# Seven block products in place of eight in the first SwiGLU product, its input normalized beforehand and its result sent through DRAM

## The chip, the cores and the metric

One core of one Trainium2 chip. TensorE (PE) multiplies 128x128 tiles, VectorE (DVE), ScalarE (ACT) and GpSimd (POOL) do the elementwise work, SyncE (SP) issues the DMAs. The metric is the device time of one execution in microseconds (us); lower is better. One median is given for several runs, and one more execution was profiled.

## What is computed

One step of a decoder layer for 1024 prompt positions and 8 sample positions, 1032 columns in all (T). The part that matters is its second half, the feed-forward network behind the mixer, all in float32:

```python
# Layer: x -> x + RMSNorm_post(Mixer(RMSNorm_pre(x))) -> h + RMSNorm_post(SwiGLU(RMSNorm_pre(h)))
def swiglu(x, w_ffn_in, w_ffn_out):
    hcat = x @ w_ffn_in                                  # 1024 -> 2 * 2816
    gate, up = hcat[..., :FFN_HIDDEN], hcat[..., FFN_HIDDEN:]
    return (jax.nn.silu(gate) * up) @ w_ffn_out          # 2816 -> 1024

yp = yp + rmsnorm(mix, norm_mix_post[l])
yp = yp + rmsnorm(swiglu(rmsnorm(yp, norm_ffn_pre[l]), w_ffn_in[l], w_ffn_out[l]), norm_ffn_post[l])
```

## The kernel before

Everything lies transposed: the 1024 model features are 8 tiles of 128 partitions (`KT`), the 1032 positions are columns. To keep float32 accuracy every operand is split into a high part and a low part (`hi`, and `lo = x - hi`, both in the type fp32r), and each product is three matmuls: high by high, weight low by input high, weight high by input low. The splits are done by ACT (the cast, line 156) and DVE (the subtraction, line 157).

The 2816 hidden features are 22 tiles (`HT`). For hidden tile t, `ffn_in` computes a gate product `pg` and an up product `pu`, each a sum over 8 feature tiles times 3 matmuls, for three column chunks `CH` of 344. That is 2 x 8 x 3 x 3 = 144 matmuls of 344 columns for a tile. The evacuation scales both by the column's norm factor `rf` (the input `fh`, `fl` is not divided by the norm; the factor is applied behind the product), takes silu, multiplies, and splits the result into `hh` and `hl` in on-chip memory. After each group of six tiles (the last has four) `ffn_out` multiplies them by the output weights and adds to `fac`; so first and second product alternate.

Ahead of this stands the stage of the norms: for each column chunk, the attention part of the mixer's output projection is added to `mix`; a sum of squares over partitions (the `nps` matmul with `ones`, followed by a square root on ACT and a reciprocal on DVE, line 191) gives the norm; `mix` becomes h, goes to `h_d`, and a second sum of squares gives `rf`. For chunk 2 the state-space part of the projection (eight `gemm` calls with `cc=(2,)`) comes first. POOL does part of the multiplications, of the sums and of the weight splits here.

The order of instructions on each engine is fixed when the program is built: by the priorities `prio(...)` and a scheduler; each engine then runs its own queue strictly in that order and waits at semaphores. SP issues all DMAs in one queue, among them 91 copies of about 1 MB from the key/value caches to the outputs, handed out by `next_copy` at the pace `RATE`.

## Time and profile before

| | |
|---|---|
| runs: median (lowest to highest of 3) | 1928.76 us (1927.81 to 1932.84) |
| the profiled execution's own time | 1929.59 us |
| its span in the trace | 1927.8 us |
| lying around the span | 1.8 us |
| granted clock of TensorE, mean | 0.979 |
| busy TensorE, VectorE, ScalarE, GpSimd | 95%, 53%, 38%, 20% of the span |

The span runs from the first to the last instruction of the trace. Matmuls are pipelined, so a matmul's own duration is longer than the distance from its start to the next one's start; it is this distance that adds up, and the text calls it the step of a matmul. A granted clock of 1.00 is 2.4 GHz, 0.50 is 1.2 GHz.

### The profile page before, as it was taken

How to read it: one execution, taken by the hardware profiler on the slowest of the kernel's cores; microseconds unless marked ns; L12 is line 12 of the kernel's file. 1: busy time of each engine (PE TensorE's matmuls, PEld its weight loads, DVE VectorE, ACT ScalarE, POOL GpSimd, SP SyncE). 2: the span in 40 equal slices, each digit the busy share in tenths (PEclk: the TensorE clock that was granted, in tenths of full speed). 3: DMA queues.
4: the chain of work that ended last, by engine and by line, in shares of the span. 5: the costliest groups of instructions: out<-in, count | busy, mean ns of one | idle time of the engine just before them, and what ended most of it. 6: DMA issues, size and time to landing. Idle time of an engine off the chain costs nothing. (4 is left out here: it accounts for less than half of the span.)

```text
span 1927.8 us, 29260 instructions
## 1 busy us (share of the span) xinstructions
PE 1825.0 (95%) x11727; PEld 1709.3 (89%) x11727; DVE 1014.0 (53%) x1896; ACT 739.2 (38%) x1388; POOL 394.5 (20%) x277
## 2 busy tenths in 40 slices
PE   8999989999999899998879989999999999999994
PEld 6999878888888798887679989999999999999993
DVE  6544676757764544455774896331333333333348
ACT  5543554545554455665242353222221112211242
POOL 0000244543232311133533342000000000000025
PEclk9999999999999999999889999999999999999997
DMA  4322333443334433464754454347433643366362
GB/s 162 122 95 86 119 108 112 137 128 107 104 115 136 156 100 110 142 237 137 178 154 133 147 168 132 109 150 249 133 115 130 240 164 131 105 202 207 115 247 88
DMA packets 125544, 275.26 MB, mean 143 GB/s; under 512 B 17616, under 2 KB 83632, under 8 KB 124000
## 3 DMA queue, kind: packets, MB, share of 16 engines
q1 hardware_dynamic: 125408, 273.39, 43.4%
q8 instruction: 92, 1.51, 0.3%
q14 instruction: 44, 0.36, 0.1%
HBM read 235.86 MB, written 125.47 MB: 187 GB/s over the span
## 5 line engine op out<-in xcount | busy, mean ns | idle before, releaser
L168 PE MATMUL g<-xh,wh 128*128 128x344 f32 x1344 | 443.7, 330 | 9.7 <-ACT zt L893 5.5
L168 PE MATMUL g<-xl,wh 128*128 128x344 f32 x1344 | 440.4, 328 | 1.5 <-DVE xl L222 1.5
L168 PE MATMUL g<-xh,wl 128*128 128x344 f32 x1344 | 439.0, 327 | 0.5 <-DVE wl L157 0.5
L168 PEld LDWEIGHTS g<-xh,wh 128*128 128x128 f32 x1344 | 255.8, 190 | 19.3 <-ACT zt L893 6.1
L168 PEld LDWEIGHTS g<-xh,wl 128*128 128x128 f32 x1344 | 256.2, 191 | 11.3 <-issue 9.9
L168 PEld LDWEIGHTS g<-xl,wh 128*128 128x128 f32 x1344 | 256.3, 191 | 10.4 <-issue 7.4
L157 DVE TENSOR_TENSOR wl<-wr,wh 128x1024 fp32r<-128x1024 f32 (+1 forms) x133 | 163.0, 1226 | 124.9 <-ACT wh L156 124.7
L156 ACT CAST wh<-wr 128x1024 fp32r<-128x1024 f32 (+1 forms) x133 | 134.4, 1011 | 214.5 <-PE g L168 128.8
L168 PE MATMUL pg<-fh,wl 128*128 128x344 f32 x504 | 161.8, 321 | 0.2 <-DVE wl L157 0.2
L168 PE MATMUL pg<-fl,wh 128*128 128x344 f32 x504 | 161.8, 321 | 0.0
L168 PE MATMUL pu<-fl,wh 128*128 128x344 f32 x504 | 161.6, 321 | 0.0
L168 PE MATMUL pu<-fh,wh 128*128 128x344 f32 x504 | 161.2, 320 | 0.0
L168 PE MATMUL pu<-fh,wl 128*128 128x344 f32 x504 | 160.8, 319 | 0.0
L168 PE MATMUL pg<-fh,wh 128*128 128x344 f32 x504 | 158.5, 322 | 0.0
L1110 POOL TENSOR_TENSOR ow<-wr,ow 128x512 fp32r<-128x512 f32 x8 | 11.1, 1407 | 674.9 <-ACT ow L1109 674.9
L168 PE MATMUL g<-hl,wh 128*128 128x344 f32 x432 | 138.0, 319 | 0.0
L168 PE MATMUL g<-hh,wl 128*128 128x344 f32 x432 | 137.6, 319 | 0.0
L168 PE MATMUL g<-hh,wh 128*128 128x344 f32 x432 | 137.3, 320 | 0.0
L230 DVE TENSOR_TENSOR u<-pu,rf 128x344 f32<-128x344 f32 x66 | 34.1, 516 | 195.5 <-PE pu L168 195.5
L650 ACT ACTIVATE sm<-sm,ngm 128x128 f32<-128x128 f32 (+1 forms) x192 | 84.9, 443 | 108.3 <-DVE ngm L646 106.2
L606 POOL TENSOR_TENSOR sw<-sw,sin 128x1032 f32<-128x1032 f32 x24 | 74.9, 3122 | 247.6 <-ACT sw L605 184.1
L1079 ACT CAST hh<-s 128x344 fp32r<-128x344 f32 x66 | 31.7, 480 | 199.4 <-DVE s L1078 197.3
(323 smaller groups left out, 3710.7 us busy)
## 6 DMA issues: line engine op xcount, KB each, us to landing
out_skv<-in_cache SPq DMA_DIRECT2D x64, 1023.5 KB, 5.3
wr<-in_w_in SPq DMA_DIRECT2D x56, 512.0 KB, 3.8
wr<-in_w_fin SPq DMA_DIRECT2D x44, 512.0 KB, 3.8
out_skv<-in_cache SPq DMA_DIRECT2D x16, 1022.0 KB, 5.5
wr<-in_w_out SPq DMA_DIRECT2D x24, 512.0 KB, 4.1
wr<-in_w_fout SPq DMA_DIRECT2D x24, 384.0 KB, 4.2
e<-cs_d SPq DMA_DIRECT2D x16, 512.0 KB, 3.9
n_d<-nh SPq DMA_DIRECT2D x12, 512.0 KB, 4.2
```

Source lines behind the costliest of these rows:

```text
L156: nc.scalar.copy(wh[:, :cols], wr[:, :cols])
L157: nc.vector.tensor_tensor(out=wl[:, :cols], in0=wr[:, :cols], in1=wh[:, :cols], op=ALU.subtract)
L168: nc.tensor.matmul(ps, x[:, ws], y[:, c0:c1], start=(k == 0 and j == 0), stop=(k == n - 1 and j == 2))
L230: return nc.vector.tensor_tensor(out=dst, in0=ps, in1=r[:dst.shape[0], c0:c1], op=ALU.mult)
L606: nc.gpsimd.tensor_tensor(out=sw[:, 0:T], in0=sw[:, 0:T], in1=sin, op=ALU.mult)
L650: nc.scalar.activation(out=sm[:, h, :nk], in_=sm[:, h, :nk], func=AF.Exp, scale=SCALE, bias=ngm[:, g, j, i:i + 1], accum_out=den[:, g, j, ...
L1079: nc.scalar.copy(hh[:, c0:c1], s)
L1110: nc.gpsimd.tensor_tensor(out=wl, in0=src, in1=wh, op=ALU.subtract)
```

## The change

Tiles 0 and 1 keep the plain products (`plain`). For tiles 2 to 21 the 2 x 2 block product (gate and up rows, lower and upper half of the features, two neighbouring column blocks A and B of `HB` = 258) is done by a scheme with seven block products instead of eight: b11, b21, t2, b22, t3, t4, t1. Each is 4 feature tiles x 3 matmuls of 258 columns, and it is done for two column halves s, so a tile is 7 x 12 x 2 = 168 matmuls of 258 columns. The scheme needs sums of input blocks and of weight blocks. The input's sums are made once, in place in `mix` (`x_sums`, `x_last`). The weights' sums are made for each tile (`w_blocks`): four sums of 512 columns, and three and a half splits instead of two. The seven results are combined by adds while they leave PSUM (`blocks`), over eight banks in turn.

For that the input has to be normalized before the product, so `Norms` divides by the second norm first, and `fh`, `fl` are made after it; `GAP` says behind how many units of TensorE's work the two norm matmuls of a chunk stand. POOL has no part in the norms any more. The result of a tile goes to DRAM (`hid_d`); `hid_load` fetches and splits it for the second product, whose four groups now stand together at the end. `RATE` for the cache copies goes from 0.52 to 0.43; 76 of them are handed out in the feed-forward part, as before.

```diff
 NEG = -1e30
 SCALE = 0.125
 
@@ -112,6 +114,12 @@
...
-    h_d = [dtile(f"h_d{k}", [P, T]) for k in range(KT)]
+    h_d = dtile("h_d", [KT, P, T])
+    hid_d = [dtile(f"hid_d{t}", [P, T]) for t in range(HT)]
...
-    for c, (c0, c1) in enumerate(CH):
-        if c == 2:
...
+    class Norms:
+
+
+        def __init__(self, c):
+            self.c0, self.c1 = CH[c]
+            self.acc = np_.tile([P, CW], F32, tag="nacc", name="nacc")
+
+        def part(self, m, ps):
+            mv = mix[m][:, self.c0:self.c1]
+            r = nc.vector.tensor_tensor(out=mv, in0=mv, in1=ps, op=ALU.add)
+            stat(mv, m == 0, self.acc)
+            return r
...
+        def first(self, prev):
+            c0, c1 = self.c0, self.c1
+            with prio("evac"):
+                r = np_.tile([P, CW], F32, tag="nr", name="nr", bufs=1)
+                finish(self.acc, r, prev=prev)
...
+                    self.h += [x[:, j] for j in range(n)]
+                    for m in range(3 * i, 3 * i + n):
+                        mv, h = mix[m][:, c0:c1], self.h[m]
+                        nc.vector.tensor_tensor(out=mv, in0=mv, in1=r, op=ALU.mult)
+                        nc.vector.scalar_tensor_tensor(out=h, in0=mv, scalar=nw(MIX_POST, m), in1=h, op0=ALU.mult,
+                                                       op1=ALU.add)
+                        stat(h, m == 0, self.acc)
+                    nc.sync.dma_start(out=h_d[3 * i:3 * i + n, :, c0:c1].rearrange("k p t -> p k t"), in_=x[:, :n])
...
+        def second(self, prev):
+            c0, c1 = self.c0, self.c1
+            with prio("evac"):
+                r = np_.tile([P, CW], F32, tag="nr", name="nr2", bufs=1)
+                finish(self.acc, r, prev=prev)
+                for m in range(KT):
+                    mv = mix[m][:, c0:c1]
+                    nc.vector.scalar_tensor_tensor(out=mv, in0=self.h[m], scalar=nw(FFN_PRE, m), in1=r, op0=ALU.mult,
+                                                   op1=ALU.mult)
+                    nc.scalar.copy(fh[m][:, c0:c1], mv)
+                    nc.vector.tensor_tensor(out=fl[m][:, c0:c1], in0=mv, in1=fh[m][:, c0:c1], op=ALU.subtract)
+
...
+    def att_part(c):
+        nm = Norms(c)
         for m in range(KT):
...
             ps = gps()
-            unit(ps, [x[:, (m % 2) * 512:(m % 2 + 1) * 512] for x in pair], ahs, als, c)
+            last = unit(ps, [x[:, (m % 2) * 512:(m % 2 + 1) * 512] for x in pair], ahs, als, c)
             with prio("evac"):
-                ev(c, ps)
+                nm.part(m, ps)
+            step(last, .5)
+        ahead.extend([(GAP[c][0], nm.first), (GAP[c][1], nm.second)])
+
+    att_part(0)
+    att_part(1)
+    for m in range(KT):
+        step(gemm(a["w_out"][m][:, 512:1536], 1024, sh, sl, ssm_ev(m), cc=(2,), share=True))
+    att_part(2)
+    right.close()
...
+    def plain(t, c, w):
+        c0, c1 = CH[c]
...
-    fst = ExitStack()
-    hhp = pool(fst, "hhp", 6, side="right")
-    hlp = pool(fst, "hlp", 6, side="right")
-    tmp = pool(fst, "tmp", 2, side="right")
+            s = np_.tile([P, T], F32, tag="fs", name="fs", bufs=2)[:, :CW]
+            nc.scalar.activation(out=s, in_=pg, func=AF.Silu)
+            next_copy(nc.vector.tensor_tensor(out=s, in0=s, in1=pu, op=ALU.mult))
+            nc.sync.dma_start(out=hid_d[t][:, c0:c1], in_=s)
+        step(last, 2)
...
+    def x_raw(s):
+        a0 = 2 * s * HB
+        A, B = slice(a0, a0 + HB), slice(a0 + HB, a0 + 2 * HB)
+        half[s, "b11"] = [(fh[k][:, A], fl[k][:, A]) for k in range(4)]
+        half[s, "b21"] = [(fh[4 + k][:, A], fl[4 + k][:, A]) for k in range(4)]
+        half[s, "b22"] = [(fh[4 + k][:, B], fl[4 + k][:, B]) for k in range(4)]
+
...
+        with prio("evac"):
+            for k in range(4):
+                x, y = mix[k], mix[4 + k]
+                nc.vector.tensor_tensor(out=x[:, A], in0=x[:, B], in1=x[:, A], op=ALU.subtract)
+                nc.vector.tensor_tensor(out=x[:, B], in0=y[:, B], in1=x[:, B], op=ALU.subtract)
+                nc.vector.tensor_tensor(out=y[:, B], in0=y[:, B], in1=x[:, A], op=ALU.subtract)
+                nc.vector.tensor_tensor(out=y[:, A], in0=y[:, A], in1=y[:, B], op=ALU.subtract)
+            split("t2", 4, B)
+            split("t3", 0, B)
+            split("t4", 4, A)
+
+    def x_last(s):
+
+        a0 = 2 * s * HB
+        A, B = slice(a0, a0 + HB), slice(a0 + HB, a0 + 2 * HB)
+        with prio("evac"):
+            for k in range(4):
+                nc.scalar.copy(fh[k][:, B], mix[k][:, A])
+                nc.vector.tensor_tensor(out=fl[k][:, B], in0=mix[k][:, A], in1=fh[k][:, B], op=ALU.subtract)
+        half[s, "t1"] = [(fh[k][:, B], fl[k][:, B]) for k in range(4)]
...
+    wslots = [(mixp, "mix")] * 8 + [(whp, "wh"), (wlp, "wl"), (whp, "wh"), (wlp, "wl")]
...
+    banks = [(psg, "g"), (psa, "ap"), (pss, "sp"), (pst, "ap"), (psg, "g"), (psa, "ap"), (pss, "sp"), (psn, "ap")]
...
+            def slot():
+                p, tag = wslots[nws[0] % len(wslots)]
+                nws[0] += 1
+                return p.tile([P, 1024 if p in (whp, wlp) else T], F32R, tag=tag, name="wsl")
+
+            def split(n0, n1, x):
+                wh, wl = slot(), slot()
+                nc.scalar.copy(wh[:, :1024], x)
+                nc.vector.tensor_tensor(out=wl[:, :1024], in0=x, in1=wh[:, :1024], op=ALU.subtract)
+                res[n0] = (wh[:, :512], wl[:, :512])
+                res[n1] = (wh[:, 512:1024], wl[:, 512:1024])
...
+            split("b11", "b21", g)
+            nc.vector.tensor_tensor(out=s1, in0=a21, in1=a22, op=ALU.add)
+            sub(s2, s1, a11)
+            split("t1", "t2", sa[:, :1024])
+            sub(s3, a11, a21)
+            sub(s4, a12, s2)
+            split("t3", "b22", sb[:, :1024])
+            w = slot()
+            nc.scalar.copy(w[:, :512], a22)
+            nc.vector.tensor_tensor(out=w[:, 512:1024], in0=a22, in1=w[:, :512], op=ALU.subtract)
+            res["t4"] = (w[:, :512], w[:, 512:1024])
+        return res
...
+    def blocks(t, s, w):
+        def prod(name):
...
+            with prio("main"):
+                for k, (hi, lo) in enumerate(half[s, name]):
+                    ks = slice(k * P, (k + 1) * P)
+                    for j, (x, y) in enumerate(((wh, hi), (wl, hi), (wh, lo))):
+                        nc.tensor.matmul(ps, x[:, ks], y, start=(k == 0 and j == 0), stop=(k == 3 and j == 2))
+            return ps
...
+        p = np_.tile([P, 4, HB], F32, tag="xr", name="fp", bufs=3)
+        o_ = np_.tile([P, 4, HB], F32, tag="fs", name="fo", bufs=2)
+        p1, u2, v, u3 = (p[:, i] for i in range(4))
+        gate, up = o_[:, 0:2], o_[:, 2:4]
+        b = prod("b11")
+        with prio("evac"):
+            nc.scalar.copy(p1, b)
+        b = prod("b21")
+        with prio("evac"):
...
+        b = prod("t1")
+        with prio("evac"):
+            add(gate[:, 1], v, b)
+            add(up[:, 1], u3, b)
+            nc.scalar.activation(out=gate, in_=gate, func=AF.Silu)
+            nc.vector.tensor_tensor(out=up, in0=up, in1=gate, op=ALU.mult)
+            nc.sync.dma_start(out=hid_d[t][:, 2 * s * HB:(2 * s + 2) * HB], in_=up.rearrange("p i t -> p (i t)"))
...
-    def ffn_weights(t, far):
-        if not far:
...
-    def ffn_in(ts, order):
...
-            with prio("evac"):
-                s = tmp.tile([P, LW], F32, tag="s", name="s")[:, :CW]
-                u = tmp.tile([P, LW], F32, tag="u", name="u")[:, :CW]
-                scaled(s, pg, c, rf)
-                last = nc.scalar.activation(out=s, in_=s, func=AF.Silu)
-                scaled(u, pu, c, rf)
-                nc.vector.tensor_tensor(out=s, in0=s, in1=u, op=ALU.mult)
-                nc.scalar.copy(hh[:, c0:c1], s)
-                nc.vector.tensor_tensor(out=hl[:, c0:c1], in0=s, in1=hh[:, c0:c1], op=ALU.subtract)
-                next_copy(last)
...
+    hslots = [(tx, "tx")] * 12 + [(actp, "act")] * 16
...
+    def hid_load(t):
+        with prio("w"):
+            hr = np_.tile([P, T], F32, tag="xr", name="hr", bufs=3)
+            nc.sync.dma_start(out=hr, in_=hid_d[t])
...
+                res.append(p.tile([P, T], F32R, tag=tag, name=f"h{'hl'[i]}{t}"))
+            nc.scalar.copy(res[0], hr)
+            nc.vector.tensor_tensor(out=res[1], in0=hr, in1=res[0], op=ALU.subtract)
+        hid[t] = res
...
+    pw = [(load_w(a["w_fin"][0], 1024), load_w(a["w_fin"][HT], 1024)), (far_weights(1), far_weights(HT + 1))]
+    for t, c in ((0, 0), (0, 1), (1, 0), (1, 1)):
+        plain(t, c, pw[t])
+    assert not ahead
+    for s in range(2):
+        x_raw(s)
+        x_sums(s)
+    for t in range(2):
+        plain(t, 2, pw[t])
+    for s in range(2):
+        x_last(s)
+    for t in range(2, HT):
+        w = w_blocks(t)
+        for s in range(2):
+            blocks(t, s, w)
+    fac = [mixp.tile([P, T], F32, tag="mix", name=f"fac{m}") for m in range(KT)]
     for gi, (t0, t1) in enumerate(groups):
-        if gi == 0:
-
-            ffn_in((0, 1), [(0, 0), (0, 1), (1, 0), (1, 1), (0, 2), (1, 2)])
-        for t in range(2 if gi == 0 else t0, t1):
-            ffn_in((t,), [(t, c) for c in range(3)])
+        for t in range(t0, t1):
+            hid_load(t)
         ffn_out(gi)```

What the build makes of it on the engines, at three places.

The first is VectorE's queue within one hidden tile, well inside the first product. Before, `s` and `u` are the scaled gate and up products, `wl` a weight split, `hl` the split of the result; these rows are one column chunk with the weights of the next tile:

```order
L230 TENSOR_TENSOR s<-pg,rf 128x344
L157 TENSOR_TENSOR wl<-wr,wh 128x1024
L230 TENSOR_TENSOR u<-pu,rf 128x344
L1078 TENSOR_TENSOR s<-s,u 128x344
L157 TENSOR_TENSOR wl<-wr,wh 128x1024
L1080 TENSOR_TENSOR hl_13421<-s,hh_13420 128x344
```

Now, about half a tile of the same queue: `fb` is a block product in PSUM, `fp` and `fo` the partial results, `sa` and `sb` the weight sums, `wsl` a weight split:

```order
L1211 TENSOR_TENSOR fp<-fp,fb 128x258 x3
L1185 TENSOR_TENSOR sa<-wu 128x512
L1182 TENSOR_TENSOR sb<-wg,wu 128x512
L1177 TENSOR_TENSOR wsl<-wg,wsl 128x1024
L1211 TENSOR_TENSOR fo<-fp,fb 128x258
L1182 TENSOR_TENSOR sa<-sa,wg 128x512
L1211 TENSOR_TENSOR fo<-fp,fb 128x258 x2
L1182 TENSOR_TENSOR sb<-wg,sa 128x512
L1211 TENSOR_TENSOR fo<-fp,fb 128x258
L1177 TENSOR_TENSOR wsl<-sa,wsl 128x1024
L1240 TENSOR_TENSOR fo<-fo 128x516
```

The work on a tile's weights stands between the adds of another tile's products, one to two tiles ahead of its use.

The second is TensorE's queue at the last norm matmul, the second one of chunk 2 (`nps`). Before, it stands in an up product of tile 1 (`wxh`, `wxl` are that tile's weights), and nothing but the scaling of results needs it:

```order
L168 MATMUL pu<-fh_10005,wxh_10991 128x344
L168 MATMUL pu<-fh_10005,wxl_10992 128x344
L990 MATMUL nps<-nacc_10878,ones 128x344
L168 MATMUL pu<-fl_10013,wxh_10991 128x344
L168 MATMUL pu<-fh_10006,wxh_10991 128x344
```

Now it stands inside the gate product of tile 1 for chunk 1, after 18 of its 24 matmuls:

```order
L176 MATMUL pg<-fl_10027,wxh 128x344
L1001 MATMUL nps<-nacc_10980,ones 128x344
L176 MATMUL pg<-fh_10020,wxh 128x344
L176 MATMUL pg<-fh_10020,wxl 128x344
L176 MATMUL pg<-fl_10028,wxh 128x344
```

Behind it in the queue are the rest of that unit, its up product, and the four units of chunk 2, whose input needs this norm.

The third is VectorE's queue ahead of that matmul, whose operand `nacc_10980` is the sum of squares of h. In the kernel before the same stretch holds splits and products, and no sums of input blocks:

```order
L1024 SCALAR_TENSOR_TENSOR fl_10013<-mix_9518,par,fh_10005 128x344
L1078 TENSOR_TENSOR s<-s,u 128x344
L1024 SCALAR_TENSOR_TENSOR fl_10014<-mix_9519,par,fh_10006 128x344
L230 TENSOR_TENSOR s<-pg,rf 128x344
L1080 TENSOR_TENSOR hl_10999<-s,hh_10998 128x344
L230 TENSOR_TENSOR u<-pu,rf 128x344
L191 RECIPROCAL rf<-rf 128x344
```

Now the splits of the first half's sums (`xt2`, `xt3`, `xt4`) stand between its first and its last six adds:

```order
L1127 TENSOR_TENSOR xt3l<-mix_9528,xt3h 128x258
L997 TENSOR_TENSOR nacc_10980<-nacc_10980,sq 128x344
L1127 TENSOR_TENSOR xt3l<-mix_9529,xt3h 128x258
L1127 TENSOR_TENSOR xt3l<-mix_9530,xt3h 128x258
L1127 TENSOR_TENSOR xt4l<-mix_9531,xt4h 128x258
L1127 TENSOR_TENSOR xt4l<-mix_9532,xt4h 128x258
L1127 TENSOR_TENSOR xt4l<-mix_9533,xt4h 128x258
L1127 TENSOR_TENSOR xt4l<-mix_9534,xt4h 128x258
L997 TENSOR_TENSOR nacc_10980<-nacc_10980,sq 128x344 x6
L1103 TENSOR_TENSOR fs<-fs,pu 128x344 x2
L201 RECIPROCAL nr_11136<-nr_11136 128x344
```

So the norm of chunk 2 stands behind the block sums of the first half in VectorE's queue.

## Rows read from the trace of the kernel before

**Rows 1.** the page: span, and TensorE's busy time with its share and instructions
```profile
span 1927.8 us, 29260 instructions
...
PE 1825.0 (95%) x11727; PEld 1709.3 (89%) x11727; DVE 1014.0 (53%) x1896; ACT 739.2 (38%) x1388; POOL 394.5 (20%) x277
```

**Rows 2.** the chain of waits: start us, length us, engine, tile, line, instructions
```profile
1193.35 3.78 PE pg L168 x24
...
1283.92 67.74 PE g L168 x432
...
1849.43 23.36 PE g L168 x132
```

**Rows 3.** busy time by stretch (the first line names the columns)
```profile
core 0: us, PE busy (x) PEld busy (x) DVE busy (x) ACT busy (x) POOL busy (x), PEclk, DMA share, GB/s
1048.00:1194.00 146.00, 133.61 (x800) 130.13 (x799) 120.91 (x154) 66.28 (x113) 57.44 (x41) 0.96 0.47 151
1194.00:1284.00 90.00, 90.00 (x574) 90.00 (x574) 32.03 (x55) 18.43 (x32) 0.00 (x0) 1.00 0.31 105
...
1849.00:1928.00 79.00, 51.09 (x297) 49.24 (x295) 56.60 (x75) 30.12 (x57) 36.38 (x31) 0.82 0.48 181
```

**Rows 4.** timeline of TensorE at the end: start us, us, instruction
```profile
1879.98 0.34 PE L168 MATMUL g<-hl,ow 128*128 128x388 f32 x1
...
1883.68 0.34 PE L168 MATMUL g<-hl,ow 128*128 128x388 f32 x1
...
1891.00 0.80 PE L168 MATMUL g<-hh,ow 128*128 128x256 f32 x2 [4.15 <-DVE fac L1123]
...
1897.46 0.28 PE L168 MATMUL g<-hl,ow 128*128 128x256 f32 x1
...
1902.74 0.28 PE L168 MATMUL g<-hl,ow 128*128 128x256 f32 x1
1913.14 1.22 PE L990 MATMUL nps<-facc,ones 128*128 128x256 f32 x2 [10.12 <-DVE facc L1129]
```

**Rows 5.** busy time of TensorE in two stretches (x: matmuls), granted clock last but two
```profile
1897.46:1902.74 5.28, 5.28 (x47) 1.00 0.00 0
1891.60:1895.44 3.84, 3.84 (x19) 0.50 0.45 155
```

**Rows 6.** groups by line and shape: us busy, ns of one, idle before
```profile
L157 DVE TENSOR_TENSOR wl<-wr,wh 128x1024 fp32r<-128x1024 f32 x109 | 140.0, 1284 | 74.7 <-ACT wh L156 74.5
...
L156 ACT CAST wh<-wr 128x1024 fp32r<-128x1024 f32 x109 | 114.4, 1049 | 110.6 <-PE g L168 38.9 <-PE pu L168 37.8 <-PE pg L168 33.1
...
L1080 DVE TENSOR_TENSOR hl<-s,hh 128x344 fp32r<-128x344 f32 x66 | 34.4, 521 | 22.9 <-ACT hh L1079 22.9
...
L458 DVE TENSOR_TENSOR hs<-hs,tm 128x512 f32<-128x512 f32 x16 | 11.0, 690 | 13.2 <-POOL tm L454 13.2
...
L190 ACT ACT_TABLE_LOAD x4 | 5.1, 1283 | 0.1
```

**Rows 7.** timeline of VectorE in the stage of the norms
```profile
1070.06 0.92 DVE L1001 TENSOR_TENSOR mix<-mix,g 128x344 f32<-128x344 f32 x2
...
1071.88 2.29 DVE L191 RECIPROCAL nr<-nr 128x344 f32<-128x344 f32 x1
...
1157.70 4.58 DVE L1020 TENSOR_TENSOR mix<-mix,nr 128x344 f32<-128x344 f32 x4
1162.20 1.54 DVE L1021 SCALAR_TENSOR_TENSOR mix<-mix,par,xr 128x344 f32<-128x344 f32 x3
```

**Rows 8.** timeline of VectorE at the end
```profile
1900.70 0.74 DVE L1123 TENSOR_TENSOR fac<-fac,g 128x256 f32<-128x256 f32 x2
```

**Rows 9.** what TensorE waited for from 1050 to 1195: us, times, longest
```profile
PE nps L990 <- POOL nacc L986: 3.2, 1, 3.2
```

**Rows 10.** DMA issues from 1194 on: count, KB, median us to landing
```profile
wr<-in_w_fin SPq DMA_DIRECT2D x36, 512.0 KB, 3.6
...
hres<-h_d SPq DMA_DIRECT2D x8, 516.0 KB, 9.7
```

More of the change, by code (lines that the diff above doesn't have):

```diff
@@ L977, in trunk, with stat @@
     fl = [actp.tile([P, T], F32R, tag="act", name=f"fl{k}") for k in range(KT)]
-    rf = rowp.tile([P, T], F32, tag="row", name="rf")
-    def stat(x, first, acc, eng):
+    def stat(x, first, acc):
         if first:
@@ L983, in stat, with finish @@
         else:
-            sq = np_.tile([P, CW], F32, tag="sq", name="sq")
+            sq = np_.tile([P, T], F32, tag="fs", name="sq", bufs=2)[:, :CW]
             nc.scalar.activation(out=sq, in_=x, func=AF.Square)
-            eng.tensor_tensor(out=acc, in0=acc, in1=sq, op=ALU.add)
-    def finish(acc, dst, cw=CW):
+            nc.vector.tensor_tensor(out=acc, in0=acc, in1=sq, op=ALU.add)
+    def finish(acc, dst, cw=CW, prev=None):
         sp_ = side_ps("nps")
-        nc.tensor.matmul(sp_[:, :cw], ones, acc, start=True, stop=True)
+        ins = nc.tensor.matmul(sp_[:, :cw], ones, acc, start=True, stop=True)
+        if prev is not None:
+            behind(ins, prev)
@@ L998, in trunk, with step @@
+    ahead = []
+    def step(last, n=1):
+        ahead[:] = [(k - n, f) for k, f in ahead]
+        while ahead and ahead[0][0] <= 0:
+            ahead.pop(0)[1](last)
+    def att_part(c):
+        nm = Norms(c)
         for m in range(KT):
-            def ev(c, ps, m=m, acc=acc):
-                r = nc.vector.tensor_tensor(out=mix[m][:, c0:c1], in0=mix[m][:, c0:c1], in1=ps, op=ALU.add)
-                stat(mix[m][:, c0:c1], m == 0, acc, nc.vector)
-                return r
             if m % 2 == 0:
```

147 lines of the change are left out of this document (90 added, 57 removed).

## The prediction, made blind

> **What bounds the kernel now.** I read the page first: TensorE is busy for 95% of a span of 1927.8 us [rows 1]. A high busy share alone proves little, because matmul durations overlap; so next comes the chain of waits. From 1193.35 to 1849.43, where the first and second products alternate, it consists of TensorE alone: two units of 24 matmuls after each other without a gap, then 432 matmuls in 67.74 us, and so on [rows 2]. The busy time by stretch says the same: from 1194 to 1284 TensorE is busy 90.00 of 90 us at clock 1.00, VectorE only 32 of 90 [rows 3]. So each matmul taken out of the first product is worth its step, as long as nothing else becomes late. The two stages around it are different. From 1048 to 1194, the stage of the norms, TensorE has holes and VectorE is busy for 121 of 146 us. The end, from 1849 on, hangs on VectorE and GpSimd [rows 3, 4].
>
> **What the product costs, before and after.** Four tiles took from 1193.35 to 1283.92 us [rows 2]: 90.57 us, 22.64 us a tile, which is 0.157 us for each of 144 matmuls of 344 columns. The change runs 168 matmuls of 258 columns. There is no row with 258, but there are neighbours at full clock. With 388 columns, 21 steps lie between 1879.98 and 1883.68: 0.176 us each. With 256, 45 steps lie between 1897.46 and 1902.74: 0.1173 us each [rows 4]; the clock there is 1.00 [rows 5]. The slope between them is 0.446 ns a column, and it gives 0.1566 for 344, which fits. So 258 columns cost 0.1182 us and a tile 19.86 us. Twenty tiles: 397.2 instead of 452.9 us, a **gain of 55.7 us**. That is nearly the full eighth, because almost the whole step goes with the columns.
>
> A fixed cost for each matmul would speak against more and shorter matmuls. The rows leave about 3 ns of it. The Trainium skill (TensorE: Matmul & The Clock Gate, Part 3, The mechanism) says that a weight load runs beside a matmul only when the two use different row groups, which full 128-row loads never do. By that rule every step would carry its load and the seven products would win far less or lose; the trace does not agree, since a step of 0.1173 us with a load each shows the load covered.
>
> **Does VectorE keep up in a tile?** Its queue for one tile holds 14 adds from PSUM of 258 columns (0.37 us each back to back [rows 8], for 256), two multiplications of 516 and four weight sums of 512 (0.69 [rows 6]), three splits of 1024 (1.28 [rows 6]) and one of 512 (0.69): 5.2 + 1.4 + 2.8 + 3.8 + 0.7 = 13.9 us of 19.9. ScalarE has 3.5 casts (1.05 each [rows 6]), two copies and two silus, under 7 us. The weight work stands one to two tiles ahead in the queue, and eight banks hold 8 x 1.43 us of results, so I put the edit's sums, splits and adds at nothing: TensorE covers them. Without that cover each microsecond over 19.9 costs 20 us. The two loads of a tile land in 3.6 us [rows 10], once in 20 us.
>
> **The stage of the norms.** Here the change adds to the engine that is already short. Up to the first norm of chunk 0 the queues are the same; its reciprocal starts at 1071.88 [rows 7], and one add more stands ahead of it: 1072.4. From it to the first weight split of tile 2 (`wsl<-wg`) I count VectorE's queue: 109 two-operand instructions of 344 columns (0.46 us back to back [rows 7]) 50.1 us; 48 with a scalar (0.51 [rows 7]) 24.5; 60 of 258 columns, nearly all block sums and their splits (0.37 [rows 8]) 22.2; 13 weight splits of 1024 (1.28 [rows 6]) 16.6; 6 reciprocals (2.29 [rows 7]) 13.7; 4 weight sums (0.69) 2.8. Sum 129.9 us, so 1202.3 without any wait. The mean step matters: before, multiplications cost 4.58 us for four while GpSimd ran [rows 7]; now GpSimd is out of the norms, and I take the undisturbed step.
>
> The waits: VectorE's second reciprocal of chunk 1 waits for its `nps`, which stands behind the first units of tile 0, about 2.7 us. The last `nps` waits for the six adds behind the block sums; 101 of the 129.9 us lie up to them, so they are done near 1176. TensorE arrives near 1159: the weights of tile 0 are split near 1129, three pairs of units of 7.5 us and 18 matmuls follow, and the input of chunk 1 holds it for some 4 us. So TensorE stands for some 17 us, where before its wait at such a matmul was 3.2 us [rows 9]. It loses its clock for the next few us (at clock 0.50 a step of 256 columns was 3.84/18 = 0.213 [rows 5]), and behind the `nps` ScalarE needs two table loads (1.28 each [rows 6]) and a square root before the reciprocal: 3 us more. Then chunk 2 is normalized (12 us), TensorE follows with its four units, and the second half's sums run beside them. First block product at about 1202.3 + 2.7 + 3 = **1208** instead of 1193.4: **14.6 us lost**. The bounds: 1201, if the waits lie beside each other, and 1220, if the waits cost as much again as TensorE lacked in this stage before (133.6 of 146 us busy [rows 3], 12.4).
>
> **The way through DRAM.** Stores go out beside the products. When the last tile ends, hidden tiles 0 and 1 are already split; the load of tile 5 waits for a buffer, lands some 4 us later (a load of this size took 3.6 to 9.7 [rows 10]), and its split (1.05 + 1.28) is done 9 us after the end. TensorE has 5.5 us of work with tiles 0 and 1 in five open units, and 2.4 us with each further one. I take **3 us** of holes, between 0 and 9. Later groups load ahead. Before, the two products alternated and this seam did not exist.
>
> **The end.** The second product's last group is the same (78.4 us from 1849.43 to the span's end). The residual's tiles 4 to 7 can only be loaded when `ow` buffers come free, so some adds of chunk 0 move behind those of chunk 2. The hole of 4.15 us that they made [rows 4] shrinks, and they come back between 1902.74 and the last `nps` at 1913.14. I take 0, between -4 and +5.
>
> **Sum** against the profiled execution's own 1929.6 us: -55.7 + 14.6 + 3 + 0 = -38.1, so **1891 us**, 2.0% below; the median of the runs, 1928.8, is 0.8 lower than that execution.
>
> **The rivals.** *A lighter transition* (15%): the norms stage ends by 1201 or sooner, because GpSimd no longer slows VectorE, and the end gains its 4 us. Time 1929.6 - 55.7 + 8 + 3 - 4, about 1881. For it: GpSimd was busy for 57 of the 146 us of that stage [rows 3]. *A heavier transition or small holes in every tile* (20%): the stage ends at 1220 and 0.3 us a tile is lost at banks or casts: 1929.6 - 55.7 + 27 + 6 + 3, about 1910. For it: the weight splits already waited 74.7 us for ScalarE's casts [rows 6], and four stand in each tile's queue now. *VectorE becomes the bound of the first product* (5%), slower than before: every split at the head of VectorE's queue waits for a cast, and that for a slot that a later product frees, so the adds behind it hold the banks. It decides from 19.86 + 38/20 = 21.8 us a tile; at 22.5 the time is 1891 + 53 = 1944. Against it: 13.9 us of work. *The step does not shrink with the columns* (2%): 168 x 0.157 = 26.4 us a tile, 1891 + 20 x 6.5 = 2021. The 256-column steps speak against it; the skill's rule on loads named above would push this way. *Nothing visible* (3%): gain and seams cancel, 1929.
>
> **From these to the numbers.** The main case has 55% and its own range 1883 to 1900. The range 1872 to 1912 takes in the lighter case and the heavier one up to a little beyond its time; it leaves out the far side of the heavier case, the three last rivals and a little below, some 2 in 10. Within 0.3% means within 5.8 us of the median, about what a measurement of this kernel can tell. Faster: main, lighter and heavier cases, 0.90; same 0.03; slower 0.07.
>
> **What would show it.** In the changed profile: `fb` matmuls of 258 columns, 3360 of them in 397 us without gaps (a tile 19.9 us); VectorE busy about 70% there; a hole of TensorE at an `nps` of more than 10 us, released by VectorE's `nacc`; the first `fb` at about 1208; and from the last `fb` to the end some 285 us (3 + 3 x 67.7 + 78.4). I am wrong if the `fb` stretch is much longer than 400 us with TensorE waiting for `wsl` or for banks, or if the stage of the norms ends beyond 1220.

## The result, and the profile after the change

The changed kernel takes **1903.3 us** (median of 4 runs, 1900.4 to 1907.3) against 1928.3 for the kernel before in the same session: ratio 0.987, 95% interval 0.984 to 0.989. It is 25.0 us faster, 1.3%; 38 were forecast. The profiled execution is the slowest of the four, 1907.3 us with a span of 1905.4. Its page, whose lines answer to [rows 1]:

```profile
span 1905.4 us, 30773 instructions
...
PE 1781.1 (93%) x12207; PEld 1662.1 (87%) x12207; DVE 1148.8 (60%) x2223; ACT 783.9 (41%) x1436; POOL 350.0 (18%) x242
```

480 matmuls more than before, 44 us less of busy TensorE. The chain of waits of the changed kernel (start, length, engine, tile or table load, line, instructions), from the end of the norms on, answers to [rows 2]:

```profile
1184.52 1.28 ACT L1102
1185.82 0.47 ACT fs L1102
1186.33 4.66 PE pg L176 x18
1190.99 0.58 PE nps L1001 x2
...
1217.82 403.18 PE fb L1207 x3357
...
1639.70 208.00 PE g L176 x1305
...
1866.68 0.58 PE g L176 x3
1867.26 9.36 DMA hres<-h_d
...
1890.64 1.23 PE nps L1001 x2
```

The twenty tiles are one piece of 403.18 us on TensorE alone. Ahead of it and at the end the chain changes engines every few microseconds, through ScalarE, VectorE and a load. Busy time by stretch (columns as in [rows 3]), the stage of the norms, the block products and the seam:

```profile
1150.00:1218.00 68.00, 43.22 (x233) 40.74 (x232) 58.76 (x132) 33.23 (x71) 0.00 (x0) 0.82 0.28 95
1218.00:1621.00 403.00, 403.00 (x3359) 403.00 (x3359) 263.13 (x480) 113.78 (x162) 0.00 (x0) 1.00 0.51 175
1621.00:1640.00 19.00, 18.03 (x113) 17.46 (x113) 11.06 (x12) 11.04 (x15) 0.00 (x0) 1.00 0.93 291
```

What TensorE waited for in the changed kernel (us in total, times, longest), two rows of the norms and one of the end:

```profile
PE pg L176 <- ACT fs L1102: 18.4, 1, 18.4
PE nps L1001 <- DVE nacc L997: 1.5, 1, 1.5
...
PE nps L1001 <- DVE facc L1309: 15.7, 2, 15.4
```

The long wait of the norms is not at the last `nps`. It stands at a plain unit (`pg`) that waits for a silu on ScalarE.

From these rows the difference of the two profiled executions adds up (spans, 1905.4 - 1927.8 = -22.4):

| part | before | after | forecast | measured |
|---|---|---|---|---|
| to the first norm's reciprocal | 1071.9 | 1076.5 | +0.5 | +4.6 |
| from it to the steady block products | 121.5 | 141.3 | +14.1 | +19.8 |
| twenty tiles | 452.9 | 403.2 | -55.7 | -49.7 |
| seam through DRAM | none | 1.0 | +3 | +1.0 |
| the end (the rest) | | | 0 | +1.9 |

The reciprocals of VectorE in the changed kernel from which the first rows come, the first one of the stage and the second one of chunk 1:

```profile
1076.48 2.30 DVE L201 RECIPROCAL nr<-nr 128x344 f32<-128x344 f32 x1
...
1148.94 2.30 DVE L201 RECIPROCAL nr<-nr 128x344 f32<-128x344 f32 x1
```

The first row of the table is scatter of the program ahead of the change. In the traces of the experiments whose code up to there does the same, that reciprocal starts between 1067.0 and 1076.3; the profiled execution is late in it. That may be most of its 4 us over its own median; the other executions have no trace that would show it.

### The profile page after: what moved, and what is told of

Its sections match the earlier page's. It is cut to its first block, busy times and chain, and to the rows that moved or that the text cites. A ratio compares the mean times of both kernels' runs of the same rounds, so it can differ in the third digit from the quotient of the medians.

```text
span 1905.4 us, 30773 instructions
## 1 busy us (share of the span) xinstructions
PE 1781.1 (93%) x12207; PEld 1662.1 (87%) x12207; DVE 1148.8 (60%) x2223; ACT 783.9 (41%) x1436; POOL 350.0 (18%) x242
## 4 chain that ended last, share of the span: by engine, by line
PE 36%; DVE 8%; DMA 4%; issue 1%; ACT 1%; POOL 1%; SPq 0%; DVEq 0%; POOLq 0%; ACTq 0%
PE fb L1207 21%; PE g L176 14%; DMA nt<-n_d 2%; PE pg L176 1%; POOL nt L856 1%; DVE xr L1034 1%; DVE nacc L997 1%; DVE wl L165 1%; DMA hres<-h_d 0%; DMA hr<-hid_d 0%; PE pu L176 0%; DVE fac L1330 0%; DMA cvt<-in_cache 0%; DVE mix L1046 0%; DVE nt L858 0%
## 5 line engine op out<-in xcount | busy, mean ns | idle before, releaser
L176 PE MATMUL g<-xh,wh 128*128 128x344 f32 x1344 | 443.7, 330 | 4.7 <-ACT rw L587 3.4
L176 PE MATMUL g<-xl,wh 128*128 128x344 f32 x1344 | 441.1, 328 | 1.5 <-DVE xl L232 1.5
L176 PE MATMUL g<-xh,wl 128*128 128x344 f32 x1344 | 439.7, 327 | 0.5 <-DVE wl L165 0.5
L176 PEld LDWEIGHTS g<-xh,wh 128*128 128x128 f32 x1344 | 256.2, 191 | 14.1 <-ACT rw L587 5.7
L176 PEld LDWEIGHTS g<-xh,wl 128*128 128x128 f32 x1344 | 256.5, 191 | 13.2 <-issue 11.8
L176 PEld LDWEIGHTS g<-xl,wh 128*128 128x128 f32 x1344 | 256.8, 191 | 9.7 <-issue 6.8
L1207 PE MATMUL fb<-fh,wsl 128*128 128x258 f32 x1280 | 234.6, 283 | 0.9 <-DVE wsl L1177 0.7
L1207 PEld LDWEIGHTS fb<-fh,wsl 128*128 128x128 f32 x1280 | 198.0, 189 | 1.5 <-DVE wsl L1177 0.9
L1207 PE MATMUL fb<-fl,wsl 128*128 128x258 f32 x640 | 180.8, 283 | 0.0
L165 DVE TENSOR_TENSOR wl<-wr,wh 128x1024 fp32r<-128x1024 f32 (+1 forms) x93 | 111.7, 1201 | 83.8 <-ACT wh L164 83.5
L176 PE MATMUL g<-hh,wh 128*128 128x344 f32 x432 | 137.4, 320 | 0.7 <-ACT wh L164 0.7
L176 PE MATMUL g<-hh,wl 128*128 128x344 f32 x432 | 137.7, 319 | 0.2 <-DVE wl L165 0.2
L176 PE MATMUL g<-hl,wh 128*128 128x344 f32 x432 | 137.3, 320 | 0.0
L1289 POOL TENSOR_TENSOR ow<-wr,ow 128x512 fp32r<-128x512 f32 x8 | 10.1, 1296 | 684.8 <-ACT ow L1288 684.8
L164 ACT CAST wh<-wr 128x1024 fp32r<-128x1024 f32 (+1 forms) x93 | 92.6, 996 | 102.0 <-PE g L176 94.9
L1207 PEld LDWEIGHTS fb<-fl,wsl 128*128 128x128 f32 x640 | 120.9, 189 | 0.0
L616 ACT COPY sw<-rw 32x1032 f32<-32x1032 f32 x96 | 101.1, 1053 | 1.4
L1211 DVE TENSOR_TENSOR fo<-fp,fb 128x258 f32<-128x258 f32 x160 | 63.9, 421 | 58.0 <-PE fb L1207 55.6
L587 ACT COPY rw<-g 128x344 f32<-128x344 f32 x108 | 47.3, 444 | 112.2 <-PE g L176 72.0
L176 PEld LDWEIGHTS g<-hh,wh 128*128 128x128 f32 x432 | 80.9, 188 | 1.1 <-ACT wh L164 1.0
## 6 DMA issues: line engine op xcount, KB each, us to landing
out_skv<-in_cache SPq DMA_DIRECT2D x64, 1023.5 KB, 5.6
wr<-in_w_in SPq DMA_DIRECT2D x56, 512.0 KB, 3.7
wr<-in_w_out SPq DMA_DIRECT2D x24, 512.0 KB, 3.7
hr<-hid_d SPq DMA_DIRECT2D x22, 516.0 KB, 4.8
wg<-in_w_fin SPq DMA_DIRECT2D x20, 512.0 KB, 5.4
wu<-in_w_fin SPq DMA_DIRECT2D x20, 512.0 KB, 3.5
```

The source lines that it names most:

```text
L164: nc.scalar.copy(wh[:, :cols], wr[:, :cols])
L165: nc.vector.tensor_tensor(out=wl[:, :cols], in0=wr[:, :cols], in1=wh[:, :cols], op=ALU.subtract)
L176: last = nc.tensor.matmul(ps, x[:, ws], y[:, c0:c1], start=(k == 0 and j == 0), stop=(k == n - 1 and j == 2))
L587: return nc.scalar.copy(rw[:, c0:c1], ps)
L616: nc.scalar.copy(sw[q * 32:(q + 1) * 32, 0:T], rw[s * 32:(s + 1) * 32, :])
L1207: nc.tensor.matmul(ps, x[:, ks], y, start=(k == 0 and j == 0), stop=(k == 3 and j == 2))
```

## The experiments

The scatter is as large as some effects. So the experiments are read in two intervals of their traces, measured from inside: from the second reciprocal of chunk 1 to the start of the last block product (471.8 us in the changed kernel: 1148.94 to 1620.70), and from there to the end of the span (284.7). These intervals scatter too: the changed kernel and e1, whose code is the same up to the last block product, differ by 0.9 us in the first; the changed kernel, e2, e3, e6 and e9, whose code is the same in the end, lie between 282.3 and 284.7 in the second (e7, at 289.1, is told below). All are edits of the changed kernel.

| run | to the last block product | from it to the end | median us | ratio to before (95%) |
|---|---|---|---|---|
| changed kernel | 471.8 | 284.7 | 1903.3 | 0.987 (0.984 to 0.989) |
| e1, residual's buffers | 472.7 | 281.0 | 1897.8 | 0.985 (0.983 to 0.988) |
| e2, sums behind the norm | 472.2 | 283.5 | 1902.2 | 0.987 (0.985 to 0.988) |
| e3, sums on GpSimd | 468.3 | 284.0 | 1900.2 | 0.986 (0.984 to 0.987) |
| e8, four mends | 467.0 | 273.7 | 1889.3 | 0.980 (0.978 to 0.982) |
| e9, squares apart | 468.2 | 282.3 | 1897.7 | 0.984 (0.982 to 0.985) |
| e11, mends with GpSimd | 462.4 | 275.8 | 1885.8 | 0.976 (0.974 to 0.979) |
| e12, mends without | 460.7 | 273.8 | 1881.1 | 0.975 (0.972 to 0.978) |

**Order of the sums (e2).** All of them stay on VectorE; those of the first half move behind the norm of chunk 2 (`behind` sets the order on one engine).

```diff
-                nc.vector.tensor_tensor(out=x[:, A], in0=x[:, B], in1=x[:, A], op=ALU.subtract)
+                behind(nc.vector.tensor_tensor(out=x[:, A], in0=x[:, B], in1=x[:, A], op=ALU.subtract), order[0])
...
```

> Only the order on VectorE changes: the input sums of the first half stand behind the second norm of chunk 2 instead of ahead of its last adds. Theory A (VectorE's whole work up to the first block product decides, wherever the sums stand): the last nps comes some 10 us earlier, near 1181, but the 10.1 us of sums then stand between it and the first weight split; first block product again at 1213 to 1219, time within 5 us of 1905. Theory B (the sums hurt only because they stand ahead of those adds; behind them TensorE's four units of chunk 2 cover them): first block product near 1207, time about 1895.

Measured: 0.4 us longer to the last block product. The last `nps` in the chain of this run, and TensorE's wait at the first weight splits:

```profile
1178.85 0.59 PE nps L1001 x2
```
```profile
PE fb L1207 <- ACT wsl L1176: 8.1, 2, 7.6
```

The last `nps` stands 33.0 us behind the second reciprocal of chunk 1 (1145.89 here) instead of 42.0, so it came 9 us sooner; and TensorE lost 8.1 of them again at the first weight split, whose buffers (`mix`, the first eight of `wslots`) are free only when all sums are done. The forecast's way of counting, the whole queue of VectorE up to that split, holds; its place in the queue only moves the hole.

**The sums on GpSimd (e3).** `eng` is GpSimd for the first half, VectorE for the second.

```diff
-        a0 = 2 * s * HB
+        eng, a0 = (nc.vector if s else nc.gpsimd), 2 * s * HB
...
-                nc.vector.tensor_tensor(out=x[:, A], in0=x[:, B], in1=x[:, A], op=ALU.subtract)
+                eng.tensor_tensor(out=x[:, A], in0=x[:, B], in1=x[:, A], op=ALU.subtract)
...
```

> The input sums of the first half and their low parts move from VectorE to GpSimd, which does nothing from 1150 to 1218; the casts of these sums stand behind the squares of chunk 2 on ScalarE. Theory A (VectorE's work up to the first block product decides): 10.1 us leave VectorE, the last nps comes near 1181, the first block product near 1208, time about 1897. Theory B (GpSimd beside VectorE slows it down as much as it takes off, as with the four multiplications that took 4.58 us): first block product at 1215 or later, time 1903 to 1908.

Measured: 3.5 us shorter, a third of the 10.1 us taken off. The same eight multiplications on VectorE, in the changed kernel with GpSimd idle:

```profile
1166.94 3.51 DVE L1033 TENSOR_TENSOR mix<-mix,nr 128x344 f32<-128x344 f32 x8
```

and in this run with GpSimd's adds beside them:

```profile
1160.44 6.97 DVE L1033 TENSOR_TENSOR mix<-mix,nr 128x344 f32<-128x344 f32 x8
```

They took twice the time. And a part was lost on ScalarE: the last `nps` came 32.5 us behind the second reciprocal of chunk 1 (1175.91), 9.4 sooner than in the changed kernel, but behind it ScalarE had casts of the sums, silus and two table loads to do before the square root:

```profile
1176.37 1.28 ACT L1102
...
1180.93 1.28 ACT L200
1182.23 0.56 ACT nr L200
```

So the reciprocal started 6.9 us behind that `nps`, in the changed kernel 1.4. Both theories are part of it: VectorE's work decides, and GpSimd takes back much of what it takes off; ScalarE's order, which neither names, takes its share.

**Squares in places of their own (e9).** The code has two buffers (`fs`) in turn for the squares of the norms and for the silus of the plain tiles. Here the squares of chunk 2's second norm go elsewhere.

```diff
-                        stat(h, m == 0, self.acc)
+                        stat(h, m == 0, self.acc, fl[m][:, c0:c1] if c1 == T else None)
...
```

> The squares of chunk 2's second norm are written into the part of the low input tiles that is still unused, one place each (rounded to the format of those tiles), instead of into the two buffers that they share with the silus of the plain tiles. Theory A (sharing these two buffers puts the silus behind all squares on ScalarE, and so holds the banks of TensorE's next units): the wait of 18.4 us for a silu goes, TensorE does its 7.5 us of units ahead of the last nps, which follows the last add; the first block product comes 62 to 65 us after the second reciprocal of chunk 1 instead of 68.9; time about 1898. Theory B (VectorE's adds end last anyway, and the units only change places with the wait): 67 us or more, time 1902 to 1905.

Measured: 3.6 us shorter. The 68.9 us run from 1148.94 to 1217.82 in the changed kernel, from where its last block product starts 402.9 us later; the first interval less 402.9 us is the count for the other runs, and it gives 65.3 here, at the far end of theory A's 62 to 65; time 1897.7. On ScalarE the two silus now start at 1164.95, ahead of the squares (in the changed kernel at 1185.82):

```profile
1164.95 0.81 ACT L1102 ACTIVATE fs<-pg 128x344 f32<-128x344 f32 x2 [6.29 <-PE pg L176]
```

TensorE's timeline has the hole where I had forecast it:

```profile
1185.66 1.51 PE L1001 MATMUL nps<-nacc,ones 128*128 128x344 f32 x2 [10.16 <-DVE nacc L997]
```

So in the changed kernel the banks were held by silus that stood behind squares for a buffer, and 5 us of plain units (4.66 us in the chain above) came behind the hole instead of into it.

**The residual's buffers (e1).** In the forecast I had the late loads wait for `ow` buffers. The chain says otherwise: the load of 9.36 us starts behind the group's last matmul (`PE g`, 1866.68), since `hres` 4 to 7 reuse the buffers of hidden tiles 20 and 21.

```diff
-                h = actp.tile([P, T], F32, tag="act", name=f"hres{m}")
+                h = (actp.tile([P, T], F32, tag="act", name=f"hres{m}") if m < 4 else tx.tile([P, T], F32, tag="tx", name=f"hres{m}"))
```

> Only the buffers of the residual's tiles 4 to 7 change: they no longer reuse those of hidden tiles 20 and 21, which the very last matmul still reads, but those of tiles 14 and 15, free one group earlier. Theory A (the late loads make the end longer): the wait of 9.36 us for a residual tile leaves the chain, the hole ahead of the last nps shrinks from 15.4 us to 6 to 9, and the execution gets 6 to 9 us shorter, about 1896 to 1898. Theory B (VectorE's own work bounds the end, busy 43.7 of the last 58 us, and the wait only fills a pause): less than 3 us. The stage of the norms and the block products stay as they are, first block product near 1218.

Measured: 3.7 us less in the end (1.3 less than the shortest end without the edit), between the two theories; the hole ahead of the last `nps` went from 15.4 to 10.5. The rest has another cause, and two timelines of this run show it, VectorE and GpSimd with four multiplications each:

```profile
1845.58 4.64 DVE L1330 TENSOR_TENSOR fac<-fac,fr 128x388 f32<-128x388 f32 x4
```
```profile
1844.87 4.93 POOL L1330 TENSOR_TENSOR fac<-fac,fr 128x388 f32<-128x388 f32 x4 [28.63 <-DVE fr L201]
```

**256 columns (e4).** This run, a single execution, is for the step alone.

```diff
-                        nc.tensor.matmul(ps, x[:, ks], y, start=(k == 0 and j == 0), stop=(k == 3 and j == 2))
+                        nc.tensor.matmul(ps, x[:, ks], y[:, :256], start=(k == 0 and j == 0), stop=(k == 3 and j == 2))
...
```

> Every block product is computed for 256 of its 258 columns; the last two columns of each block are left out (and set to zero), so that matmuls have the width of the row from which I took the step. Theory A (the step goes with the columns at 0.45 ns each, and the row of 45 steps was a quicker place): step 0.119 us, the 3360 matmuls take 400 us instead of 403.2. Theory B (258 columns cost something that 256 do not): step 0.1173 as in that row, 394 us.

Its chain:

```profile
1217.63 400.21 PE fb L1207 x3357
```

0.1192 us a step: theory A. A matmul of 256 columns costs 1.6% more in this stretch than the 0.1173 of [rows 4]; the two columns more cost 0.0009. Why the two places differ I didn't find out; both have the granted clock 1.00.

**More work for VectorE in the product (e6, e7).** The three large weight splits of a tile are made two or three times; each run is a single execution.

```diff
-                nc.vector.tensor_tensor(out=wl[:, :1024], in0=x, in1=wh[:, :1024], op=ALU.subtract)
+                for _ in range(2):
+                    nc.vector.tensor_tensor(out=wl[:, :1024], in0=x, in1=wh[:, :1024], op=ALU.subtract)
```

> In every tile of the block products VectorE makes each of the three large weight splits twice, with the same result: 3.66 us more a tile, 13.1 to about 16.8 of the 20.16 us of TensorE. Theory A (VectorE's work of the product is covered): the 3360 matmuls take 403 us as before, time 1900 to 1907. Theory B (its place in the queue already costs: adds behind a split hold banks): at least 0.5 us a tile, 413 us or more.

> The same splits three times: 7.3 us more a tile, 20.4 us of VectorE against 20.16 us of TensorE. Theory A (VectorE becomes the bound where its work passes that of TensorE, and not much earlier): the products take 408 to 425 us, with waits of TensorE for weight splits or banks. Theory B (queue order makes it the bound earlier): more than 430 us. If they stay at 403 us, VectorE's work of a tile is smaller than I count.

Busy time from 1240 to 1600, in the changed kernel, with the splits made twice, and three times (TensorE, its weight loads, VectorE):

```profile
1240.00:1600.00 360.00, 360.00 (x3002) 360.00 (x3002) 235.03 (x431) 100.88 (x143) 0.00 (x0) 1.00 0.49 169
```
```profile
1240.00:1600.00 360.00, 360.00 (x3002) 360.00 (x3001) 290.59 (x483) 101.25 (x145) 0.00 (x0) 1.00 0.49 169
```
```profile
1240.00:1600.00 360.00, 359.65 (x3000) 359.44 (x2999) 341.28 (x533) 98.55 (x142) 0.00 (x0) 1.00 0.50 168
```

In the steady stretch almost nothing is lost (0.35 of 360 us) even with VectorE busy 95% of the time (its work is 19.1 us a tile there; I had counted 20.4, so the bound was not passed). The intervals of both runs are longer (475.2 and 480.2 us to the last block product), and most of that is in the first tile: TensorE waited 2.4 and 5.4 us there for weight splits (0.9 in the changed kernel), and behind the waits some 17 matmuls in each run took steps of 0.215 us, with a granted clock down to 0.50. For e7 the 408 to 425 us of theory A came out, 412 from the first to the last block product (404 in the changed kernel), but not by its mechanism. Its end is longer too, 289.1 us, with 2.7 us of TensorE waiting for a weight cast.

**All tiles plain (e5, e10).**

```diff
     for t in range(2, HT):
-        w = w_blocks(t)
-        for s in range(2):
-            blocks(t, s, w)
+        w = (load_w(a["w_fin"][t], 1024), load_w(a["w_fin"][HT + t], 1024))
+        for c in range(3):
+            plain(t, c, w)
```

> All 22 tiles are plain units of 344 columns (144 matmuls a tile); the block products, the input sums and the weight sums are gone; the normalized input, the two norms in one go and the way through DRAM stay. Theory A (the block products bring the whole gain, and the rest of the change costs): 20 tiles take 452.9 us instead of 403.2, the stage of the norms ends some 14 us sooner after the second reciprocal of chunk 1 than in the changed kernel, because 23 us of sums leave VectorE; about 1940 us, slower than before the change by some 10 us. Theory B (normalized input and DRAM gain by themselves, since no scaling is left in the evacuation): below 1925 us.

1954.6 us (ratio 1.014, 1.012 to 1.016), far more than either theory says, and the cause is at the start: with fewer places at which a cache copy is issued six were left over, and since nothing holds them they ran first. ScalarE's first square waits for its input until 25.63, in the changed kernel until 5.80:

```profile
25.63 1.49 ACT L224 ACTIVATE sq<-xc 128x344 f32<-128x344 f32 x3 [23.40 <-DMA xc<-in_xT]
```

The issues of its first 40 us hold the six copies, ahead of the first load of `xc`:

```profile
out_skv<-in_cache SPq DMA_DIRECT2D x6, 1023.5 KB, 12.4
```

Its time tells nothing of the block products. With the pace of before (`RATE` 0.52):

> As the run with all tiles plain, but with the pace of the cache copies of before (0.52), so that none of them is left over to run at the program's start, where six of them took 20 us. Theory A (the block products bring the whole gain and the rest costs): 1932 to 1940 us, first unit of tile 2 some 54 us after the second reciprocal of chunk 1, 20 tiles in 453 us. Theory B (normalized input and the way through DRAM gain by themselves): below 1925 us.

1933.5 us, ratio 1.003 (1.002 to 1.004): theory A. The second product begins 506.6 us behind the second reciprocal of chunk 1 (1142.06 to 1648.68), in e5 some 507. The first unit of tile 2 is in the chain:

```profile
1195.76 3.77 PE pg L176 x24
```

That is 53.7 us behind the reciprocal instead of 68.9, and the 20 tiles take 452.9. So the block sums, with what waits for them, cost 15 us of the norms, the block products give back 50, and without them the rest of the change costs 5 us against before (3 to 8 by the interval). From the second product's start to the end the changed kernel takes 284.4 us and this one 280.9, a difference somewhat above the scatter named above.

**Mends together (e8).** The end without GpSimd, the buffers of e1, the sums as in e3 with their casts behind those of chunk 2's norm, and the first weight splits in buffers that do not wait for the sums.

```diff
-OUT_POOL = ((1, 3, 5, 7), (0, 2, 4, 5, 6), (4, 6, 7))
+OUT_POOL = ((), (), ())
...
-                nc.scalar.copy(hi[:, k], x)
+                behind(nc.scalar.copy(hi[:, k], x), order["fh"])
...
-    nws = [0]
+    nws = [8]
```

> Four mends together: the residual's tiles 4 to 7 in buffers that are free early; the last multiplications and residual adds all on VectorE, since GpSimd beside it makes four of its instructions take 4.64 us instead of 1.9; the first half's input sums on GpSimd, with their casts behind those of chunk 2's second norm, so that no square and no square root on ScalarE waits for them; the first weight splits in buffers that do not wait for the input sums. Theory A (VectorE's work and ScalarE's order in the stage of the norms, VectorE's work at the end): from the second reciprocal of chunk 1 to the first block product 58 us instead of 68.9, from the last block product to the end 276 instead of 284.4; time about 1885. Theory B (GpSimd's sums slow VectorE so far that nothing is left, and the end without GpSimd is as long): 1895 to 1900, as with each mend alone.

1889.3 us, between the theories. The end fell to 273.7, better than expected: 7.3 us below e1, and GpSimd's absence is the only edit of the end that e1 has not. The stage of the norms gained only 4.8 of the 11. TensorE still waited for a silu that stood behind the squares, did the rest of its plain unit between that wait and the last `nps`, and waited once more for a weight split behind the first products:

```profile
1179.15 4.97 PE pg L176 x18
```
```profile
PE pg L176 <- ACT fs L1102: 12.5, 1, 12.5
...
PE fb L1207 <- DVE wsl L1177: 1.5, 1, 1.5
```

Ahead of that split stands something that I had not seen: GpSimd's first four low parts, with VectorE busy beside it from 1191.57 to 1208,

```profile
1192.55 16.05 POOL L1127 TENSOR_TENSOR xt2l<-mix,xt2h 128x258 fp32r<-128x258 f32 x4 [22.60 <-ACT xt2h L1126]
```

against 2.82 us for the same four in e3, where VectorE was mostly idle:

```profile
1175.51 2.82 POOL L1127 TENSOR_TENSOR xt2l<-mix,xt2h 128x258 fp32r<-128x258 f32 x4 [7.60 <-ACT xt2h L1126]
```

The shortest, median and longest of the four in e8, in ns:

```profile
L1127 POOL TENSOR_TENSOR xt2l<-mix,xt2h x4: 828/1330/12685, 1192.5 to 1206.9; 128x258 fp32r<-128x258 f32 x4
```

One took 12.69 us, while VectorE did over 30 instructions one after another without a gap. The other eight low parts came so late that they ran beside VectorE's own last ones, of which four took 3.43 us (1.43 in the changed kernel). What TensorE saw of all this is the wait of 1.5 us.

**The last two (e11, e12)** add the squares of e9 and bring the low parts back to VectorE; e12 brings the sixteen adds back too, behind the norm of chunk 2. From e11 to e12:

```diff
-        eng, a0 = (nc.vector if s else nc.gpsimd), 2 * s * HB
+        eng, a0 = nc.vector, 2 * s * HB
...
-                eng.tensor_tensor(out=x[:, A], in0=x[:, B], in1=x[:, A], op=ALU.subtract)
+                behind(eng.tensor_tensor(out=x[:, A], in0=x[:, B], in1=x[:, A], op=ALU.subtract), order["fl"])
```

> The mended kernel with the squares in places of their own, and GpSimd left with only the sixteen adds of the first half's input sums; their low parts are back on VectorE, since GpSimd's first four took 16 us beside a busy VectorE. Theory A: no wait for weight splits behind the first products; block products from 57 us after the second reciprocal of chunk 1, end as in the mended kernel (273 us), time about 1880. Theory B (the sums only find another wait): 1887 to 1890 as before.

> The same, with the sixteen adds on VectorE too, behind the second norm of chunk 2. Theory A (VectorE alone is quicker than both side by side: eight multiplications 3.5 us instead of 7.0): last nps some 5 us earlier than with GpSimd, 5.8 us of adds later in the queue, part of them beside the first products; within 3 us of the version with GpSimd. Theory B (all sums must end before the first product, as their tiles hold the buffers of the third weight split): 6 us or more longer than with GpSimd.

e11: 1885.8 us, 6 over its forecast and under theory B's 1887 to 1890, 59.5 us by the count of e9 (57 forecast), without a wait for weight splits; its first interval is 4.6 us below that of e8. e12: **1881.1 us**, ratio 0.975 (0.972 to 0.978), 57.8 us by that count, 1.7 below e11: theory A. Its block products start 53.2 us behind the reciprocal already, and TensorE then waits 2.8 us for a weight split, and behind it has a granted clock of 0.54 from 1203 to 1206. The medians of the two can't be told apart by their runs (1878.4 to 1886.0 and 1877.0 to 1886.2). Eight multiplications of the end on VectorE alone in e12:

```profile
1835.74 3.86 DVE L1330 TENSOR_TENSOR fac<-fac,fr 128x388 f32<-128x388 f32 x8
```

One engine does eight in 3.86 us; in e1 the two together needed 5.35, from 1844.87 to 1850.22 (1845.58 + 4.64).

## Why the forecast was right, and where it was too good

The direction and the mechanism held: the matmuls taken out count in full because TensorE alone sets that stretch, and the norms pay for it. Of the 38.1 us, 25.0 came by the medians and 22.4 by the spans of the profiled executions. The measured 1903.3 is inside the range of 1872 to 1912, but 12 us above the 1891 and outside the main case's 1883 to 1900: two terms, the product and the norms, were each some 6 us too good, and the other two nearly right.

- **The product: right mechanism, 6 us too much.** 3360 steps of 0.1200 us against 0.1182. The term was mis-sized by the row from which the 256-column step was taken, 45 steps in a quicker place (e4). The 344-column step was taken from the stretch itself and held. With it went the share of a step that doesn't go with the columns: 258 columns at 0.1200 us and 344 at 0.1572 (90.57 us for 576) lie on a line of 0.433 ns a column and 8 ns a matmul, where the forecast had 3. That estimate gives 0.1191 for 256 columns (0.1192 in e4) and 0.176 for 388 [rows 4]; the 0.1173 is the one row off it. The change adds 480 matmuls, so that share grows, and the gain is 49.7 us and not the full eighth of 452.9, 56.6.
- **A step that does not shrink (2021): not so.** A step fell from 0.157 to 0.1200 us with a weight load in each. The rule of the Trainium skill (TensorE: Matmul & The Clock Gate, Part 3, The mechanism), by which full 128-row loads don't run beside matmuls, does not agree with that. What the same page of the Trainium skill says in Part 2 (Step-by-step: what each phase is for), and what the forecast left out, is that a load into the background weight buffer may be pulled ahead of matmuls in flight; the measured step agrees with it, though no row shows which buffer a load fills.
- **VectorE covered in a tile: right.** 13.9 us forecast; 263.13 us in the stretch are 13.2 a tile, and e6 and e7 show the cover good up to 95%. The rival in which VectorE becomes the bound has nothing in the rows.
- **The stage of the norms: the way of counting right, the sum 5.7 us short.** From the first reciprocal to the block products 135.6 were forecast and 141.3 measured. The last add to `nacc` ends 108 us behind it (1184.46) instead of 103.6. The forecast hole of 17 us is there, 18.4, but at `pg` and not at `nps`: the step that failed is that TensorE would go on with its units up to the last `nps`. Silus behind squares held its banks (e9). That put the `nps` 6.5 us further back. Behind the `nps` it took 26.8 us to the block products instead of 32: from the last add on VectorE was busy for 24.5 us where the count had left 28.9, and the two table loads that the forecast put behind the `nps` were done before it (the reciprocal started right behind it, at 1192.19). Of the three differences (+4.4, +6.5, -5.2) the sum is 5.7.
- **The way through DRAM: right, and cheaper.** 1.0 us of holes instead of 3.
- **The end: right size, wrong cause.** +1.9 us, inside -4 to +5; that the size fits is luck. The hole of 4.15 us [rows 4] did shrink, to 1.04, and came back at the last `nps`, 15.4 instead of 10.1; but what delays the loads is the last matmul, and they are not the larger part: GpSimd beside VectorE costs twice as much (3.7 us in e1, 7.3 more in e8).

From the last block product to the end 284.7 us were measured and 285 forecast. The time, 1903.3, lies between the main case and the heavier one, whose cause (a norms stage up to 1220, small holes in each tile) is half there: the stage ended at 1217.8, the tiles have no holes, their steps are longer.

## What to carry to other kernels

When work is added to an engine that is already short, count its whole queue up to the instruction that the next stage needs; where in the queue it stands changes the place of the hole and not the time, unless buffers let the next stage start earlier. Look for buffers in turn that two kinds of work share: the later kind can wait for all of the earlier, as the silus did here, and hold its banks meanwhile. Before work goes to GpSimd to take it off VectorE, look in a trace at what VectorE's instructions take beside it; here handing work back to VectorE won 7 us at the end (e8). Take a step's price from many steps in the stretch that it is for, and measure an edit between two marks of the trace when the program ahead of it scatters.

## What the runs showed of the hardware

GpSimd and VectorE side by side were slower here than VectorE alone: multiplications of 128x388 took 1.16 us each on VectorE beside GpSimd (four in 4.64) and 0.48 alone (eight in 3.86); of 128x344 0.87 (eight in 6.97) and 0.44 (eight in 3.51). The other way round it could be worse: four GpSimd instructions took 16.05 us beside a busy VectorE, 12.69 of it a single one, and 2.82 beside a mostly idle one. The Trainium skill (SBUF — State Buffer, SBUF: two separate sides) has the two share a pair of ports that one instruction holds for its whole length, when VectorE's has two operands in SBUF and GpSimd's reads there; the rows agree with it where the two engines take turns, and each instruction seems to wait out one of the other's. The 12.69 us are longer than any VectorE instruction beside them (at most 1.22 us), so there GpSimd seems to have waited out many in a row.

A matmul of 258 columns, with the load of its weights, took 0.1200 us on average over 3360 of them, and one of 256 took 0.1173 or 0.1192 by the place, at the same granted clock of 1.00.
